# A streaming-encoder block on one Trainium2 core: the residual kept in HBM, and two pairs of buffers for the raw splits

## The chip, the cores and the metric

The kernel runs on one core of a Trainium2 chip. The metric is device time in microseconds (us) of one execution, the median of several runs. Lower is better. The engines have short names in the profile: PE is TensorE's matrix multiplication, PEld its loading of weights, DVE is VectorE, ACT is ScalarE, POOL is GpSimd, and SP (SyncE) issues nearly all of the DMA transfers.

## The reference

One encoder layer works on `x`, 256 frames of 2048 float32 values. It adds five terms to a running sum, the residual, one after the other:

```
x = x + 0.5 * swiglu(rms_norm(x, ffn1_norm), ffn1_w_gate, ffn1_w_up, ffn1_w_down)
proj = rms_norm(x, mix_norm) @ w_in
x = x + concat(pool_mixer(...), gla_mixer(...)) @ w_out
x = x + mem_cross_attention(rms_norm(x, xattn_norm), rms_norm(mem, mem_norm), w_q, w_kv, w_o)
x = x + 0.5 * swiglu(rms_norm(x, ffn2_norm), ffn2_w_gate, ffn2_w_up, ffn2_w_down)
out = rms_norm(x, final_norm)
```

`swiglu` is `(silu(h @ w_gate) * (h @ w_up)) @ w_down`, with a hidden width of 5632. All is float32, and the weights are some 400 MB that are read once each.

## The kernel before

**Units.** Every weight matrix is cut into units of 1 MB, tiles of 128x2048 float32. A unit is loaded into one of three buffers `raw`. Since TensorE is fed with a shorter type (`fp32r`), each unit is split into a high half `wh`, which ScalarE casts (L216), and a low half `wl`, which VectorE makes as the difference (L217). There are three buffers of each. Activations are split alike: `xs` holds the halves of the normed residual, `ys` those of the hidden state or of a mixer's output. One float32 product then becomes three matrix products (`products`, L284, matmul in L289): high by high, high by low, low by high. A plain unit is 24 matmuls of 128x512.

**The order.** `Stream` (L34) holds all 378 units and the small operations between them in program order. `emit` (L65) splits a unit two units ahead of its use, and when unit u is split it issues the load of unit u + 3. A small operation is put into the stream with a delay, counted in units (`op`, L55). The tile framework then plans each engine's order from this program, so the order on an engine is not always that of the program; every engine works its own queue off in order.

**Seven-product units.** Three of the eight units of a gate or up block (numbers 0, 2 and 4, `PAIRS` in L597) use a scheme with seven products in the place of eight: 21 matmuls instead of 24 (`seven`, L367, matmul in L383). It needs sums of weights, which VectorE adds into a tile `T` (`add_weights`, L341), and sums of activations, `xe` (`part_sums`, L323). `split_seven` (L352) makes `wh` and `wl` from `T`. Three of the seven products, P1, P2 and P3, use weights themselves, so a second pair of halves, `xh` and `xl`, is split from three quarters of `raw` (128x1536; these are the raw splits). There is one buffer of each. This second split is a function `rest`, which `emit` keeps in a list `late` and calls when it comes to the next unit; the load of unit u + 3 is issued only after it. In P1, P2 and P3 `xh` is used first and `xl` second. A block of such units (`block_s`, L388) takes all four PSUM tiles; at its end `combine` and `join` (L421, L432) add the seven results up in a tile `sg`.

**The stages.** FFN1 goes through the hidden width in three parts of 4, 4 and 3 blocks of 512 columns (`FF_PARTS`, L595). In each part pairs of blocks are computed, gate first and up second. After the up block the hidden state of the pair is turned: TensorE transposes it into a PSUM tile `ph` (L643), and ACT and DVE split it into `ys`. In a part with two pairs, the first pair is turned during the second pair's up block (the delay is in L658). At the end of each part the down projection adds it to the residual. The mixer follows, then its output projection, cross attention and its output projection, FFN2 in the same three parts, and the final norm.

**The residual.** `X` is one tile in SBUF, 128 partitions by 2 halves of the frames by 2048 values (L167). `load_x` (L524) fills it at the start in eight pieces between the first weight loads. `into_x` (L583) is called for every down projection but the last and for both output projections: two blocks of 1024 columns, each of which is added to `X` (`residual`, L557) from PSUM by VectorE, in two steps of 512 columns. After the last part of a stage `fold` (L566) transposes the new columns on TensorE and splits them into `xs`. `x_chunk` (L535) and `x_squares` (L546) do the same for the start. The last down projection is `down_end` (L1105): `end_evict` (L1134) adds to `X` and multiplies by the final gain into tiles `O`, which have the buffers of `sg`, and `finish` (L1151) scales the rows and stores the output.

Of the kernel before, what the change touches and what calls it, by code (L numbers as in the profile page):

```python
# [7 lines left out]
F32 = mybir.dt.float32  # L8
F32R = mybir.dt.float32r
AF = mybir.ActivationFunctionType  # L10
# [4 lines left out]
P = 128  # L15
D = 2048
S = 256
M = 256
FF = 5632
KT = D // P  # L20
NB = 512
# [71 lines left out]
def build(ctx, tc, I, out):  # L93
    nc = tc.nc
    st = Stream()
# [7 lines left out]
    scope = {"stack": None}  # L103
# [21 lines left out]
    def uid(s):  # L125
        cnt[0] += 1
        return f"{s}{cnt[0]}"
# [36 lines left out]
    sums = ctl("sums", [P, 2])  # L164
    chain = ctl("chain", [P, 2, 8])

    X = main.tile([P, 2, D], F32, tag="X", name="X")  # L167
    xs = main.tile([P, KT, 2, S], F32R, tag="xs", name="xs")
    ys = main.tile([P, KT, 2, S], F32R, tag="ys", name="ys")

# [181 lines left out]
    def split_seven(u, raw, t):  # L352
        th, tl = (
            wpool.tile([P, 4 * NB], F32R, tag=n, name=f"{n}{u}", bufs=st.AHEAD + 1)
            for n in ("wh", "wl")
        )
        split(th, tl, t)
        parts = [x.rearrange("p (b n) -> p b n", n=NB) for x in (th, tl)]

        def rest():  # L360
            r = [scope["pool"].tile([P, 3 * NB], F32R, tag=n, name=f"{n}{u}") for n in ("xh", "xl")]
            split(*r, raw[:, NB:])
            parts.extend(x.rearrange("p (b n) -> p b n", n=NB) for x in r)

        return [parts], rest

    def seven(banks, act, ext, i, g, first, later, weights):  # L367
        th, tl, rh, rl = weights
# [150 lines left out]
    def turn_gains(lo, hi):  # L519
        ps = ptile(uid("pgain"))  # L520
        nc.tensor.transpose(ps[:, 0, :P], rows["gain"], ident)
        nc.vector.tensor_copy(gains[:, lo:hi], ps[:, 0, lo:hi])

    def load_x(c):  # L524
        cols = slice(c * S, (c + 1) * S)
        nc.sync.dma_start(X[:, :, cols], I["x"][0].rearrange("(h p) d -> p h d", p=P)[:, :, cols])

    def first_load_order():
        for c in range(1, 8):
# [2 lines left out]

    first_loads = first_load_order()

    def x_chunk(c):  # L535
        v = ptile(uid("px"))[:, 0, :].rearrange("p (a b) -> p a b", a=2)
        k = 2 * c
        for j in range(2):
            for h in range(2):
                nc.tensor.transpose(  # L540
                    v[:, j, h * P : (h + 1) * P], X[:, h, (k + j) * P : (k + j + 1) * P], ident
                )
        for j in range(2):
            rows["hi", c] = split_scaled(xs, k + j, v[:, j, :], gcol(G_FFN1 + k + j))

    def x_squares(c):  # L546
        with tc.issue_after(rows["hi", c].ins):
            row_squares([X[:, h, c * S : (c + 1) * S] for h in range(2)], c)

    def more_gains():  # L550
        gain_columns(
# [2 lines left out]
             ("gla_b_a", G_BA, 4)], nc.sync,  # L554
        )

    def residual(scale, b):  # L557

        def evict(j, ps):
            x = X[:, :, (2 * b + j) * NB : (2 * b + j + 1) * NB]  # L560
            nc.vector.scalar_tensor_tensor(
                out=x, in0=ps, scalar=scale, in1=x, op0=ALU.mult, op1=ALU.add
            )
        return evict

    def fold(c, gain):  # L566

        v = four(ptile(uid("px")))
        for j in range(4):
            for h in range(2):  # L570
                nc.tensor.transpose(  # L571
                    v[:, j, h * P : (h + 1) * P],
                    X[:, h, c * NB + j * P : c * NB + (j + 1) * P], ident,
                )
        for j in range(4):
            split_scaled(xs, 4 * c + j, v[:, j, :], gcol(gain + 4 * c + j))
        for h in range(2):
            q = tmp.tile([P, NB], F32, tag="j", name=uid("j"), bufs=2)
            nc.scalar.activation(
                q, X[:, h, c * NB : (c + 1) * NB], AF.Square, accum_out=ss[:, h, c : c + 1]  # L580
            )

    def into_x(w, act, scale, gain=None, k0=0, nk=KT, spread_too=True):  # L583

        for b in range(2):
            block_t(wwide(w, b * 2 * NB, k0, nk), act, residual(scale, b))
            if gain is not None:
                for j in range(2):
                    st.op(lambda c=2 * b + j: fold(c, gain), 1)
        if gain is not None:  # L590
            st.op(lambda: finish_norm(4, spread_too), 2)
            if spread_too:
                st.op(spread_norm, 3)
# [81 lines left out]
        st.op(lambda c=c: x_squares(c), 6)  # L675
    st.op(lambda: finish_norm(8, False), 7)
    st.op(more_gains, 8)
    st.op(lambda: turn_gains(G_MIX, G_END), 20)

    def down_first(wd, k0, nk, last):  # L680
        into_x(wd, ys, 0.5, G_MIX if last else None, k0, nk)

    for g in PAIRS:
        pair_sums(g, 5)
# [408 lines left out]
    fin = {}  # L1093
# [11 lines left out]
    def down_end(wd, k0, nk):  # L1105

        acc_ps, kept = {}, []

        def mm(b, k, h, wh, wl):

            wh, wl = (w.rearrange("p (k j n) -> p k j n", j=2, n=NB) for w in (wh, wl))
            for j in range(2):
                nb = 2 * b + j
                if nb not in acc_ps:
                    acc_ps[nb] = ptile(uid("pe"))
                for kk in range(2):
                    products(acc_ps[nb][:, h, :], ys, k + kk, h, wh[:, kk, j], wl[:, kk, j],
                             k + kk == 0, k + kk == nk - 1)
                if k == nk - 2:
                    end_evict(nb, h)  # L1120

        def unit(b, k):
            def fn(wh, wl):
                for h in range(2):
                    mm(b, k, h, wh, wl)
            return fn

        def end_unit(b):
            def fn(wh, wl):
                kept.append((wh, wl))  # L1130
                mm(b, nk - 2, 0, wh, wl)
            return fn

        def end_evict(nb, h):  # L1134
            cols = slice(nb * NB, (nb + 1) * NB)
            if h == 0 and nb % 2 == 0:
                e = scope["pool"].tile([P, 4, NB], F32, tag="sg", name=uid("O"), bufs=2)
                fin[nb], fin[nb + 1] = e[:, 0:2], e[:, 2:4]
            xn, o = X[:, h, cols], fin[nb][:, h, :]
            nc.vector.scalar_tensor_tensor(  # L1140
                out=xn, in0=acc_ps[nb][:, h, :], scalar=0.5, in1=xn, op0=ALU.mult, op1=ALU.add
            )
            nc.scalar.activation(o, xn, AF.Square, accum_out=ss[:, h, nb : nb + 1])
            if nb < 3 or h == 0:
                nc.gpsimd.tensor_tensor(out=o, in0=xn, in1=fin["gB"][:, cols], op=ALU.mult)

        def row_factor(h):
            nc.vector.tensor_reduce(out=sums[:, h : h + 1], in_=ss[:, h, :4], axis=AX.X, op=ALU.add)
            rsqrt(Rcol[:, h : h + 1], sums[:, h : h + 1], D, 1)

        def finish(h, c, engine=None):  # L1151
            cols = slice(c * NB, (c + 1) * NB)
            x, o, r = fin[c][:, h, :], X[:, h, cols], Rcol[:, h : h + 1]
            if h == 1 and c == 3:
                nc.vector.scalar_tensor_tensor(
                    out=o, in0=o, scalar=r, in1=fin["gB"][:, cols], op0=ALU.mult, op1=ALU.mult
                )
            elif engine is nc.scalar:
                nc.scalar.activation(o, x, AF.Copy, scale=r)
            else:  # L1160
                nc.vector.tensor_scalar_mul(o, x, r)
            nc.sync.dma_start(out[0, h * P : (h + 1) * P, cols], o)

        def second_half():
            row_factor(0)
# [12 lines left out]

        st.op(ready_sqrt, 8)
        st.op(last_gain, 2)  # L1180
        for b in range(2):
            for i, src in enumerate(wwide(wd, b * 2 * NB, k0, nk - 2)):
                st.unit(src, unit(b, 2 * i))
        for b in range(2):
            st.unit(wwide(wd, b * 2 * NB, k0 + nk - 2, 2)[0], end_unit(b))
        st.op(second_half)
# [73 lines left out]
```

## Time and profile before

| | |
|---|---|
| three runs | median 2155.78 us, from 2154.47 to 2157.33 |
| the profiled execution | 2156.07 us |
| its span in the profile | 2154.2 us |
| mean granted clock of TensorE | 0.996 of full speed |
| DVE, wait of the `xl` split for the cast of `xh` | 3.7 us, 8 times |
| HBM | 400.80 MB read, 2.10 MB written |

The profile is of one execution. The span runs from the first to the last recorded instruction; the 1.9 us beside it lie around it. A page gives the busy time of each engine with its share of the span, the groups of instructions (line, engine, operation, tile written <- tiles read, shape, count, then busy us, mean ns of one, and the idle time just before them with what ended it) and the DMA queues (packets, MB, share of the DMA engines). Views of the trace give waits (engine, tile and line <- engine, tile and line that released it: us in total, times, longest), single instructions in order of time (start in us, length in us, then the instruction, with the idle time before it in brackets), busy time by stretches of the span, and the chain of work that ended last. Line numbers are those of the kernel. The clock in such a view is the one that the throttle granted TensorE, as a share of full speed.

### The profile page before, as it was taken

What the parts mean: (1) busy time and instruction counts of PE and PEld (TensorE: products, weight loads), DVE (VectorE), ACT (ScalarE), POOL (GpSimd) and SP (SyncE); (2) the same over time, 40 slices, a digit from 0 to 9 for tenths busy, and PEclk for the clock granted to TensorE, in tenths of its full rate; (3) what the DMA queues carried; (4) which work ended last, traced back from release to release, by engine and by line L of the source; (5) the groups of instructions that cost most, each with busy time, mean ns of one, the idle gap of its engine ahead of it and who ended that gap; (6) DMA issues with size and microseconds to landing.
All of it is one profiled execution on the core that took longest, in us unless ns stands there. A gap on an engine that the chain in (4) does not pass through costs nothing.

```text
span 2154.2 us, 23983 instructions
## 1 busy us (share of the span) xinstructions
PE 2122.0 (99%) x10032; PEld 1771.5 (82%) x10032; DVE 1428.1 (66%) x1189; ACT 1007.4 (47%) x890; POOL 14.1 (1%) x41
## 2 busy tenths in 40 slices
PE   9999999999999999999999999999999999999998
PEld 7878888788888888888888888888878887888886
DVE  8786588756865576565665545567874888658744
ACT  7453354533543545445445434445543445434433
POOL 0000000000000000000000000000000000000001
PEclk9999999999999999999999999999999999999999
DMA  7555555555565555556555555555556554665653
GB/s 274 176 195 200 210 176 192 192 189 192 188 212 186 182 170 179 172 177 198 189 182 166 168 175 157 181 190 197 174 195 195 198 193 170 201 195 197 227 181 117
DMA packets 134675, 404.44 MB, mean 188 GB/s; under 512 B 8868, under 2 KB 12040, under 8 KB 134184
## 3 DMA queue, kind: packets, MB, share of 16 engines
q1 hardware_dynamic: 134536, 402.92, 55.8%
q8 instruction: 78, 1.28, 0.2%
q14 instruction: 29, 0.24, 0.0%
q10 hardware_dynamic: 32, 0.01, 0.0%
HBM read 400.80 MB, written 2.10 MB: 187 GB/s over the span
## 4 chain that ended last, share of the span: by engine, by line
PE 92%; DVE 5%; issue 2%; ACT 1%; DMA 1%; SPq 0%; DVEq 0%; ACTq 0%
PE pt L289 54%; PE pa L274 15%; PE pt L383 10%; PE pb L289 6%; PE pe L289 3%; DVE wl L217 2%; ACT wh L216 1%; PE ph L643 1%; DVE xl L217 1%; DVE T L345 1%; PE pl L1036 1%; PE pv L1071 1%; PE px L571 0%; DVE sg L434 0%; DMA raw<-in_ffn_w_gate 0%
## 5 line engine op out<-in xcount | busy, mean ns | idle before, releaser
L217 DVE TENSOR_TENSOR wl<-raw,wh 128x2048 fp32r<-128x2048 f32 (+2 forms) x328 | 740.2, 2258 | 530.9 <-ACT wh L216 529.9
L216 ACT CAST wh<-raw 128x2048 fp32r<-128x2048 f32 (+2 forms) x329 | 618.4, 1881 | 671.7 <-PE pt L289 471.4
L289 PE MATMUL pt<-wh,xs 128*128 128x512 f32 x1952 | 616.6, 390 | 0.0
L289 PE MATMUL pt<-wh,ys 128*128 128x512 f32 x1728 | 534.6, 389 | 0.0
L289 PEld LDWEIGHTS pt<-wh,xs 128*128 128x128 f32 x1952 | 366.6, 188 | 76.0
L289 PE MATMUL pt<-wl,xs 128*128 128x512 f32 x976 | 380.6, 390 | 0.0
L289 PEld LDWEIGHTS pt<-wh,ys 128*128 128x128 f32 x1728 | 324.1, 188 | 67.0
L289 PE MATMUL pt<-wl,ys 128*128 128x512 f32 x864 | 336.4, 389 | 0.0
L274 PE MATMUL pa<-xs,wh 128*128 128x512 f32 x896 | 318.4, 399 | 1.7 <-DVE t L248 1.7
L274 PE MATMUL pa<-xs,wl 128*128 128x256 f32 x896 | 249.3, 281 | 0.0
L289 PEld LDWEIGHTS pt<-wl,xs 128*128 128x128 f32 x976 | 183.6, 188 | 37.7
L274 PEld LDWEIGHTS pa<-xs,wh 128*128 128x128 f32 x896 | 168.4, 189 | 41.0 <-issue 2.0
L216 ACT CAST wh<-T 128x2048 fp32r<-128x2048 f32 x54 | 103.1, 1909 | 190.0 <-DVE T L349 148.6
L289 PEld LDWEIGHTS pt<-wl,ys 128*128 128x128 f32 x864 | 162.2, 188 | 33.5
L217 DVE TENSOR_TENSOR wl<-T,wh 128x2048 fp32r<-128x2048 f32 x54 | 123.8, 2292 | 88.9 <-ACT wh L216 88.9
L274 PEld LDWEIGHTS pa<-xs,wl 128*128 128x128 f32 x896 | 169.8, 190 | 1.6 <-issue 0.2
L289 PE MATMUL pb<-wh,xs 128*128 128x512 f32 x384 | 121.7, 392 | 0.5 <-DVE ys L209 0.5
L383 PE MATMUL pt<-wh,xe 128*128 128x512 f32 x324 | 114.5, 394 | 2.1 <-DVE ys L217 2.1
L216 ACT CAST xh<-raw 128x1536 fp32r<-128x1536 f32 x54 | 80.0, 1482 | 52.5 <-PE pt L383 22.1
L217 DVE TENSOR_TENSOR xl<-raw,xh 128x1536 fp32r<-128x1536 f32 x54 | 94.6, 1753 | 4.0 <-ACT xh L216 3.7
L289 PEld LDWEIGHTS pb<-wh,xs 128*128 128x128 f32 x384 | 72.1, 188 | 15.6 <-DVE ys L209 0.7
L383 PE MATMUL pt<-xh,xs 128*128 128x512 f32 x216 | 80.3, 396 | 1.5 <-DVE ys L217 1.5
(202 smaller groups left out, 1674.0 us busy)
## 6 DMA issues: line engine op xcount, KB each, us to landing
raw<-in_ffn_w_down SPq DMA_DIRECT2D x88, 1024.0 KB, 5.4
raw<-in_ffn_w_up SPq DMA_DIRECT2D x80, 1024.0 KB, 5.1
raw<-in_ffn_w_gate SPq DMA_DIRECT2D x77, 1024.0 KB, 5.1
raw<-in_w_in SPq DMA_DIRECT2D x32, 1024.0 KB, 5.2
raw<-in_xattn_w_kv SPq DMA_DIRECT2D x32, 1024.0 KB, 5.3
raw<-in_w_out SPq DMA_DIRECT2D x16, 1024.0 KB, 5.6
raw<-in_xattn_w_q SPq DMA_DIRECT2D x16, 1024.0 KB, 5.1
raw<-in_xattn_w_o SPq DMA_DIRECT2D x16, 1024.0 KB, 5.7
```

What stands on the lines that cost most here:

```text
L216: nc.scalar.copy(hi, src)
L217: nc.vector.tensor_tensor(out=lo, in0=src, in1=f32(hi), op=ALU.subtract)
L274: nc.tensor.matmul(o, w, x, start=k == 0 and i == 0, stop=last and i == 1)
L289: nc.tensor.matmul(ps, a, w, start=first and i == 0, stop=last and i == 2)
L345: nc.vector.tensor_tensor(out=v[:, 0:2], in0=w[:, 1:3], in1=w[:, 0:1].to_broadcast([P, 2, NB]), op=ALU.add)
L383: nc.tensor.matmul(banks[n], x, w, start=first and j == 0, stop=not later and n in ("P1", "P5", "P6", "P7") and j == 2,)
L643: nc.tensor.transpose(v[:, i, h * P : (h + 1) * P], g[:, h, i * P : (i + 1) * P], ident)
L1036: nc.tensor.matmul(ps[:, t, :M], ys[:, 4 * h + d, a, tok], xa["K"][:, d, b, :], start=i == 0, stop=i == 11,)
L1071: nc.tensor.matmul(ps[:, d, :S], xa["V"][:, m, a, col], xa["PT"][:, m, b, :], start=i == 0, stop=i == 5,)
```

## The change

Two things change together. The residual becomes two DRAM tiles of 256 x 1024. A block of columns lives in SBUF only while it is worked on: `fetch_x` reads it into a tile with the tag `sg` (two buffers, shared with the hidden state and the sums of the seven-product blocks) by two transfers of 0.5 MB, two units into the block's own units, and `store_x` writes it back by two transfers after the second addition. The first part of FFN1 fetches from the input `x` instead. The final outputs `O` take the buffers of `xh` and `xl`. And `xh` and `xl` have two buffers each; they are split at once with `wh` and `wl` of the same unit, not later, so that `late` stays empty. One small operation is delayed by 22 units instead of 20.

```diff
-    X = main.tile([P, 2, D], F32, tag="X", name="X")
+    X = [dram.tile([S, 2 * NB], F32, tag=f"X{b}", name=f"X{b}") for b in range(2)]
...
-        def rest():
-            r = [scope["pool"].tile([P, 3 * NB], F32R, tag=n, name=f"{n}{u}") for n in ("xh", "xl")]
+        if True:
+            r = [
+                scope["pool"].tile([P, 3 * NB], F32R, tag=n, name=f"{n}{u}", bufs=2)
+                for n in ("xh", "xl")
+            ]
             split(*r, raw[:, NB:])
             parts.extend(x.rearrange("p (b n) -> p b n", n=NB) for x in r)
-        return [parts], rest
+        return [parts], None
...
+    def x_tile(b):
+        xrows[b] = scope["pool"].tile([P, 2, 2 * NB], F32, tag="sg", name=uid("x"), bufs=2)
+        return xrows[b]
...
+    def fetch_x(b, src=None):
+        t = x_tile(b)
+        for h in range(2):
+            rows_h = slice(h * P, (h + 1) * P)
+            nc.sync.dma_start(
+                t[:, h], X[b][rows_h, :] if src is None else src[rows_h, b * 2 * NB : (b + 1) * 2 * NB]
+            )
+
+    def store_x(b):
+        for h in range(2):
+            nc.sync.dma_start(X[b][h * P : (h + 1) * P, :], xrows[b][:, h])
+
     def residual(scale, b):
         def evict(j, ps):
-            x = X[:, :, (2 * b + j) * NB : (2 * b + j + 1) * NB]
+            x = x_cols((2 * b + j) * NB, NB)
             nc.vector.scalar_tensor_tensor(
                 out=x, in0=ps, scalar=scale, in1=x, op0=ALU.mult, op1=ALU.add
             )
+            if j:
+                store_x(b)
...
         for b in range(2):
+            st.op(lambda b=b: fetch_x(b, src), 2)
             block_t(wwide(w, b * 2 * NB, k0, nk), act, residual(scale, b))
...
-    st.op(lambda: turn_gains(G_MIX, G_END), 20)
+    st.op(lambda: turn_gains(G_MIX, G_END), 22)
...
-        into_x(wd, ys, 0.5, G_MIX if last else None, k0, nk)
+        into_x(wd, ys, 0.5, G_MIX if last else None, k0, nk, src=None if k0 else I["x"][0])
...
-            if h == 0 and nb % 2 == 0:
-                e = scope["pool"].tile([P, 4, NB], F32, tag="sg", name=uid("O"), bufs=2)
-                fin[nb], fin[nb + 1] = e[:, 0:2], e[:, 2:4]
-            xn, o = X[:, h, cols], fin[nb][:, h, :]
+            if h == 0:
+                t = scope["pool"].tile([P, 3 * NB], F32, tag=("xh", "xl")[nb % 2], name=uid("O"), bufs=2)
+                fin[nb] = t[:, : 2 * NB].rearrange("p (h n) -> p h n", h=2)
+            xn, o = x_cols(nb * NB, NB)[:, h], fin[nb][:, h]
...
         st.op(last_gain, 2)
+        for b in range(2):
+            st.op(lambda b=b: fetch_x(b), 1 + 2 * b)
```

More of the change, by code (lines that the diff above doesn't have):

```diff
@@ L165, in build @@
     chain = ctl("chain", [P, 2, 8])
-    X = main.tile([P, 2, D], F32, tag="X", name="X")
+    dram = ctx.enter_context(tc.tile_pool(name="dram", bufs=1, space=bass.MemoryType.DRAM))
+    X = [dram.tile([S, 2 * NB], F32, tag=f"X{b}", name=f"X{b}") for b in range(2)]
     xs = main.tile([P, KT, 2, S], F32R, tag="xs", name="xs")
@@ L522, in turn_gains @@
         nc.vector.tensor_copy(gains[:, lo:hi], ps[:, 0, lo:hi])
+    xrows = {}
+    def x_tile(b):
+        xrows[b] = scope["pool"].tile([P, 2, 2 * NB], F32, tag="sg", name=uid("x"), bufs=2)
+        return xrows[b]
     def load_x(c):
-        cols = slice(c * S, (c + 1) * S)
-        nc.sync.dma_start(X[:, :, cols], I["x"][0].rearrange("(h p) d -> p h d", p=P)[:, :, cols])
+        b = c // 4
+        if c % 4 == 0:
+            x_tile(b)
+        at = (c % 4) * S
+        nc.sync.dma_start(
+            xrows[b][:, :, at : at + S],
+            I["x"][0].rearrange("(h p) d -> p h d", p=P)[:, :, c * S : (c + 1) * S],
+        )
     def first_load_order():
@@ L533, in build, with x_cols @@
     first_loads = first_load_order()
+    def x_cols(c, n):
+        b = c // (2 * NB)
+        return xrows[b][:, :, c - b * 2 * NB : c - b * 2 * NB + n]
     def x_chunk(c):
@@ L540, in x_chunk @@
                 nc.tensor.transpose(
-                    v[:, j, h * P : (h + 1) * P], X[:, h, (k + j) * P : (k + j + 1) * P], ident
+                    v[:, j, h * P : (h + 1) * P], x_cols((k + j) * P, P)[:, h], ident
                 )
@@ L547, in x_squares @@
         with tc.issue_after(rows["hi", c].ins):
-            row_squares([X[:, h, c * S : (c + 1) * S] for h in range(2)], c)
+            row_squares([x_cols(c * S, S)[:, h] for h in range(2)], c)
     def more_gains():
@@ L555, in more_gains @@
         )
+    def fetch_x(b, src=None):
+        t = x_tile(b)
+        for h in range(2):
+            rows_h = slice(h * P, (h + 1) * P)
+            nc.sync.dma_start(
+                t[:, h], X[b][rows_h, :] if src is None else src[rows_h, b * 2 * NB : (b + 1) * 2 * NB]
+            )
+    def store_x(b):
+        for h in range(2):
+            nc.sync.dma_start(X[b][h * P : (h + 1) * P, :], xrows[b][:, h])
     def residual(scale, b):
         def evict(j, ps):
-            x = X[:, :, (2 * b + j) * NB : (2 * b + j + 1) * NB]
+            x = x_cols((2 * b + j) * NB, NB)
             nc.vector.scalar_tensor_tensor(
@@ L568, in fold @@
         v = four(ptile(uid("px")))
+        x = x_cols(c * NB, NB)
         for j in range(4):
@@ L571, in fold @@
                 nc.tensor.transpose(
-                    v[:, j, h * P : (h + 1) * P],
-                    X[:, h, c * NB + j * P : c * NB + (j + 1) * P], ident,
+                    v[:, j, h * P : (h + 1) * P], x[:, h, j * P : (j + 1) * P], ident
                 )
@@ L578, in fold, with into_x @@
             q = tmp.tile([P, NB], F32, tag="j", name=uid("j"), bufs=2)
[L579 to L583, printed above, removed]
+            nc.scalar.activation(q, x[:, h], AF.Square, accum_out=ss[:, h, c : c + 1])
+    def into_x(w, act, scale, gain=None, k0=0, nk=KT, spread_too=True, src=None):
         for b in range(2):
+            st.op(lambda b=b: fetch_x(b, src), 2)
             block_t(wwide(w, b * 2 * NB, k0, nk), act, residual(scale, b))
@@ L1152, in finish @@
             cols = slice(c * NB, (c + 1) * NB)
-            x, o, r = fin[c][:, h, :], X[:, h, cols], Rcol[:, h : h + 1]
+            x, o, r = fin[c][:, h], x_cols(c * NB, NB)[:, h], Rcol[:, h : h + 1]
             if h == 1 and c == 3:
```

## The prediction

> **What bounds the kernel now.** I read the page first, then TensorE's waits, then busy time by stretch, then the rows of one stretch. From the page:
>
> ```profile
> PE 2122.0 (99%) x10032; PEld 1771.5 (82%) x10032; DVE 1428.1 (66%) x1189; ACT 1007.4 (47%) x890; POOL 14.1 (1%) x41
> ...
> q1 hardware_dynamic: 134536, 402.92, 55.8%
> ...
> L216 ACT CAST wh<-raw 128x2048 fp32r<-128x2048 f32 (+2 forms) x329 | 618.4, 1881 | 671.7 <-PE pt L289 471.4
> ...
> raw<-in_ffn_w_down SPq DMA_DIRECT2D x88, 1024.0 KB, 5.4
> ```
>
> TensorE is busy for 2122.0 of the 2154.2 us of the span, so 32.2 us is all that any rearrangement can win by filling its gaps. The DMA engines are used to 55.8%, and the casts that fill `wh` mostly wait for TensorE to give a buffer back, not for weights. So the question is which of the 32 us are waits that this change touches. The waits, TensorE's and, for comparison, two of ScalarE's (us in total, times, longest):
>
> ```profile
> ACT xh L216 <- PE pt L383: 22.1, 18, 2.6
> ...
> ACT xh L216 <- DMA raw<-in_ffn_w_up: 19.7, 8, 3.1
> ...
> PE pt L383 <- DVE xl L217: 10.7, 5, 2.9
> ...
> PE pt L383 <- DVE ys L217: 3.6, 4, 2.1
> ```
>
> Line 383 is the matmul of the seven-product units, and `xl` is the low half of their raw splits, the tile that gets a second buffer. It is the largest wait on TensorE: 10.7 us in 5 waits, with 3.6 us more for `ys`. ScalarE's cast of `xh` waited 18 times for TensorE to finish with the single buffer, and 8 times for its weights. Busy time by stretch (columns: PE, PEld, DVE, ACT, POOL, granted clock, DMA share, GB/s) shows where:
>
> ```profile
> 100.00:160.00 60.00, 56.09 (x254) 45.48 (x253) 48.46 (x38) 32.19 (x23) 0.00 (x0) 1.00 0.50 175
> 370.00:420.00 50.00, 46.53 (x205) 37.47 (x206) 41.43 (x31) 25.32 (x19) 0.00 (x0) 0.98 0.57 195
> 1512.00:1570.00 58.00, 54.54 (x241) 43.79 (x241) 47.26 (x36) 30.64 (x22) 0.00 (x0) 0.98 0.50 170
> 1775.00:1832.00 57.00, 53.52 (x239) 42.99 (x238) 47.24 (x36) 29.71 (x22) 0.00 (x0) 0.99 0.48 167
> 160.00:272.00 112.00, 112.00 (x504) 93.01 (x503) 68.84 (x43) 44.50 (x26) 0.00 (x0) 1.00 0.57 197
> 414.80:417.60 2.80, 0.00 (x0) 0.00 (x0) 2.80 (x3) 0.00 (x0) 0.00 (x0) 1.00 0.60 152
> 418.00:421.30 3.30, 3.30 (x9) 2.61 (x8) 1.22 (x3) 2.30 (x2) 0.00 (x0) 0.50 0.98 379
> 2145.00:2154.20 9.20, 0.00 (x0) 0.00 (x0) 3.60 (x11) 2.00 (x6) 1.27 (x1) 0.69 0.61 228
> ```
>
> The first four stretches are the same place four times: the up block of a second column pair, in the first two parts of both feed-forward stages, where the hidden state of the pair before is turned as well. TensorE lacks 3.9, 3.5, 3.5 and 3.5 us in them, 14.4 together. The fifth is a down stage: TensorE never idles. The last is the tail of the kernel; the change adds nothing to its chain, so its 9.2 us stay.
>
> After the 2.90 us stall that ends at 417.62 the granted clock is 0.50 through the seventh stretch. Half speed costs half of its 3.3 us, 1.7 us, on top of the idle time. The trace's 0.98 and 0.99 in stretches two to four are the same thing once in each; the first stretch, whose stalls are 2.11 and 1.76, shows 1.00. [...]
>
> **Why TensorE waits there.** DVE, then ACT, in the second stretch; the second ACT row is the cast of `xh`:
>
> ```profile
> 385.41 2.29 DVE L217 TENSOR_TENSOR wl<-raw,wh 128x2048 fp32r<-128x2048 f32 x1 [0.15 <-ACT wh L216]
> ...
> 397.74 1.22 DVE L434 TENSOR_TENSOR sg<-pt,sg 128x1024 f32<-128x1024 f32 x1 [3.17 <-PE pt L289]
> 398.88 2.28 DVE L217 TENSOR_TENSOR wl<-T,wh 128x2048 fp32r<-128x2048 f32 x1
> ...
> 403.28 1.22 DVE L217 TENSOR_TENSOR ys<-ph,ys 128x1024 fp32r<-128x1024 f32 x1
> ...
> 410.27 2.29 DVE L217 TENSOR_TENSOR wl<-T,wh 128x2048 fp32r<-128x2048 f32 x1 [2.06 <-ACT wh L216]
> 412.48 2.28 DVE L217 TENSOR_TENSOR wl<-raw,wh 128x2048 fp32r<-128x2048 f32 x1
> 414.68 1.22 DVE L345 TENSOR_TENSOR T<-raw 128x1024 f32<-128x1024 f32 x1
> 415.81 1.75 DVE L217 TENSOR_TENSOR xl<-raw,xh 128x1536 fp32r<-128x1536 f32 x1
> ```
>
> ```profile
> 394.65 1.91 ACT L216 CAST wh<-T 128x2048 fp32r<-128x2048 f32 x1 [2.30 <-DVE T L349]
> ...
> 411.95 1.47 ACT L216 CAST xh<-raw 128x1536 fp32r<-128x1536 f32 x1
> ```
>
> ```profile
> 404.55 0.50 PE L383 MATMUL pt<-xh,xs 128*128 128x512 f32 x1 [0.52 <-DVE ys L217]
> ...
> 417.62 0.53 PE L383 MATMUL pt<-xl,xs 128*128 128x512 f32 x1 [2.90 <-DVE xl L217]
> ```
>
> While DVE idles for 3.17 us before 397.74 it could have made this `xl`, but its buffer still holds the unit before. The write comes 18 us later, behind two `wl` and a `T` (queues are in order), and TensorE stands from 414.72 to 417.62.
>
> **The change part by part.** *Second pair of xh and xl.* Instruction counts on TensorE, DVE and ScalarE are unchanged; the order is not. In the changed order of DVE the `xl` of the second seven-product unit stands before the `wl` of the first. Its weights were loaded behind the third `wl` before (about 387.6, two units back) and land after about 5.4, by 393; the cast takes 1.47, to about 394.7; `xl` 1.75, to 396.4: inside the 3.17 us in which DVE idled. The first `wl` then starts at 396.6, where its cast (394.65 to 396.56, now a little behind `xh`) ends, and not at 398.88. Running the rest of the changed order with the rows' lengths (wl 2.2, sg, T and ys 1.14 each, the short sums 0.6): sg to 399.9, wl 402.1, T 403.2, ys 404.3, sg 405.5, T ready 406.7, cast 1.9, second-unit `wl` at about 411. TensorE needs that at 414, and the `xl` is long there. So the 2.90 and its 1.7 of clock go. The 0.52 before 404.55 goes too: `ys` ends no later, and three products of the later unit are ordered ahead of the wait. That is 5.1 us. What is late next is the third unit's `wl`, at about 421.7, against a need of about 423.5. The third and fourth stretches are ordered alike and have the same rows:
>
> ```profile
> 1554.34 0.50 PE L383 MATMUL pt<-xh,xs 128*128 128x512 f32 x1 [0.49 <-DVE ys L217]
> ...
> 1567.41 0.50 PE L383 MATMUL pt<-xl,xs 128*128 128x512 f32 x1 [2.87 <-DVE xl L217]
> ...
> 1817.25 0.50 PE L383 MATMUL pt<-xh,xs 128*128 128x512 f32 x1 [0.52 <-DVE ys L217]
> 1830.32 0.50 PE L383 MATMUL pt<-xl,xs 128*128 128x512 f32 x1 [2.90 <-DVE xl L217]
> ```
>
> 0.49 + 2.87 + 1.7 and 0.52 + 2.90 + 1.7 give 5.1 and 5.1. The first stretch has two stalls:
>
> ```profile
> 142.80 0.50 PE L383 MATMUL pt<-wh,xe 128*128 128x512 f32 x1 [2.11 <-DVE ys L217]
> ...
> 155.74 0.50 PE L383 MATMUL pt<-xl,xs 128*128 128x512 f32 x1 [1.76 <-DVE xl L217]
> ```
>
> The 1.76 goes for the same reason. The 2.11 is a wait for a PSUM bank that `ys` frees; in the new order `xl` goes into an idle gap, `ys` is only some 0.4 earlier, and three more products (0.7) precede the wait: I keep 1.0 of it. That is 1.1 + 1.8 = 2.9.
>
> *What the new order costs.* ScalarE's queue is in order, and some `xh` casts now stand ahead of a `wh` cast that TensorE needs sooner. The worst place is the second pair's start in the second part:
>
> ```profile
> 365.82 2.29 DVE L217 TENSOR_TENSOR wl<-T,wh 128x2048 fp32r<-128x2048 f32 x1 [2.05 <-ACT wh L216]
> ```
>
> The `wl` at 365.82 ended at 368.1. It gets one more `xl` (1.75) and some 1.0 of waiting for that `xh` ahead of it: about 370.8. TensorE starts that pair at 356.92 and has 58 products before it needs it:
>
> ```profile
> 356.92 0.39 PE L383 MATMUL pt<-xh,xs 128*128 128x512 f32 x1
> ```
>
> ```profile
> 169.00 24.26 PE pt L289 x107
> ```
>
> By the second row (of the chain that ended last) a product takes 24.26 / 107 = 0.227, so the need is at 370.1: a new stall of 0.7, in both feed-forward stages, 1.4 in all. Bounds, by the rows: 0 where the load lands in time, 2.9 with a half-clock window (4.6) where it does not. I take 0.7, from the chain itself.
>
> *Residual in HBM.* SP issues 60 more transfers of 0.5 MB: 32 fetches and 28 stores, 31.5 MB on 402.92, so the DMA share goes from 56% to about 60% and in a down stage from 0.57 to about 0.71. Nothing on TensorE reads them directly except the transposes of the fold, a unit after the add. A fetch is issued about six units (6 x 24 x 0.227 = 33 us) before its add, against 5.4 for 1 MB: hidden. The one wait in SP's order is at the first down units: the fetch needs the buffer of the hidden state, which TensorE frees when it turns it. The SP rows (from a load's issue on) and the chain:
>
> ```profile
> 191.45 3.97 SPq L471 DMA_DIRECT2D raw<-in_ffn_w_down  x2
> ```
>
> ```profile
> 193.25 1.75 PE ph L643 x16
> ```
>
> ```profile
> 203.44 1.91 ACT L216 CAST wh<-raw 128x2048 fp32r<-128x2048 f32 x1 [3.53 <-PE pt L289]
> ```
>
> The fetch cannot go before 195.0, and the weight load issued at 191.45 is behind it: 3.6 of waiting, about 0.7 for two more issues, 1 MB ahead of it in the one queue at most 5.4, charged in full: 10 us late. It landed at about 196.9 and was cast at 203.44, for a unit that TensorE starts at about 214: cast and `wl` take 4.2, so 13 us late would be just in time. Cost taken: 0. Without that cover it would be 1 us on TensorE for each us beyond. The stores stand behind the add that feeds them, and in DVE's order the add stands before the `wl` that releases the next load, so they hold up nothing. [...]
>
> *The sum.* 2.9 + 5.1 + 5.1 + 5.1 = 18.2 won, 1.4 lost: 16.8 us. The profiled execution took 2156.07 (1.9 around its span); less 16.8 it is 2139.3. The median of the three runs shown is 2155.78, 0.3 below it. I say **2139.5**.
>
> **The rivals.**
> - *Early casts block the queue (gain halved).* If the loads behind the early `xh` casts land 2 us later than 5.4, the `wh` casts behind them move, and the start of each pair's second block stalls: 4 or 5 places with 1 to 2 us each. For: `xh` is the one cast that already waited for loads. Against: most places have 2 to 3 us of cover. 2139.5 + 8 = 2147, up to 2153.
> - *The change doesn't remove the wait.* DVE is busy for 41.43 of 50 us there; if the backlog and not the buffer is the cause, `xl` is made early and something else is late by as much, and the time is 2154 to 2157. Against: DVE's own 3.17 us of idle time just ahead.
> - *SP is held up (slower).* One mechanism: at the eight blocks of down projections that start behind a turned or freed buffer, the fetch stands at SP's head and weight loads wait. It decides from 13 us of lateness on, 3 more than worked out. At 2 us beyond it, each of 8 places loses 2 + 1.7 of clock, 30 us, against the 16.8 won: 2169. Against: the stretch 160 to 272, with TensorE full and casts that wait for TensorE.
>
> **How the numbers follow.** Forecast (2134 to 2147) 0.62; first rival (2147 to 2153) 0.15; no effect 0.10; slower 0.13. All FFN stalls gone with their clock would be 2156.07 - 14.4 - 5.1 = 2136.6; the changed schedule may also move the small gaps of the mixer by 2 us, so the low end is 2134. The high end takes in the first rival, 2153; what is left out is some 0.2. A measurement of this kernel tells about 0.2% (4.3 us) from no change: faster than that 0.75 (the forecast and most of the first rival), within it 0.12, slower 0.13.
>
> **What would show each step.** Right: TensorE's waits for `xl` and the four gaps shrink to about 1 us in each stretch, no 0.50 clock there, `xh` no longer waits for TensorE; about 434 MB in the queue. Wrong: waits of line 383 on `wl` or on the casts at the start of second blocks; weight casts that wait for DMA in the down stages; TensorE idle there at all. The prediction falls if idle time on TensorE stays above 25 us in all.

## The result, and the profile after

The changed kernel takes 2137.71 us (median of four runs, 2136.34 to 2138.64) against 2155.83 for the kernel before: a ratio of 0.9915, 95% interval 0.9898 to 0.9932. The forecast was 2139.5, with a range of 2134 to 2147. The profiled executions are 2138.64 and 2156.07, 17.4 apart, and the spans 2136.9 and 2154.2.

From the page of the changed kernel; the line numbers of the matmuls and splits are two to five higher than before (L216 and L217 are now L218 and L219, L289 is L291, L383 is L388):

```profile
PE 2115.0 (99%) x10032; PEld 1769.1 (83%) x10032; DVE 1425.8 (67%) x1189; ACT 1006.0 (47%) x890; POOL 14.2 (1%) x41
...
q1 hardware_dynamic: 143176, 434.38, 60.1%
...
HBM read 417.58 MB, written 16.78 MB: 203 GB/s over the span
```

TensorE's span minus its busy time went from 32.2 to 21.9 us, which is 10.3 of the 17.3. The other 7.0 are busy time, mostly products that no longer run at half clock: the trace of before has four windows of 0.50 ahead of its tail, each 3.41 us long, that of the changed kernel one, and three times half of 3.41 is 5.1. The queue moved the 31.5 MB more that were counted from the code. The waits of the changed kernel (us in total, times, longest):

```profile
ACT xh L218 <- DMA raw<-in_ffn_w_gate: 36.6, 16, 4.8
ACT xh L218 <- DMA raw<-in_ffn_w_up: 36.1, 19, 5.1
...
ACT xh L218 <- PE pt L388: 25.7, 6, 10.6
...
PE pt L291 <- ACT wh L218: 1.7, 2, 0.8
PE pt L388 <- DVE ys L219: 1.7, 3, 0.7
```

No wait of TensorE for `xl` is left in the list, where 10.7 us stood. The cast of `xh` is now mostly ahead of its weights: it waits 35 times for a load, and TensorE never for `xh`. One sign that the prediction named for being right did not show: the cast still waits for TensorE, 25.7 us in 6 waits, where it was 22.1 us in 18. The four stretches again (columns as before):

```profile
100.00:160.00 60.00, 59.26 (x271) 48.88 (x270) 50.86 (x40) 33.05 (x23) 0.00 (x0) 1.00 0.60 205
...
370.00:420.00 50.00, 49.46 (x226) 40.78 (x225) 42.27 (x32) 28.07 (x21) 0.00 (x0) 1.00 0.62 210
...
1512.00:1570.00 58.00, 57.62 (x263) 47.55 (x262) 48.88 (x36) 30.91 (x23) 0.00 (x0) 1.00 0.57 190
...
1775.00:1832.00 57.00, 57.00 (x260) 47.17 (x259) 49.19 (x36) 32.36 (x23) 0.00 (x0) 1.00 0.63 214
```

TensorE lacks 0.74, 0.54, 0.38 and 0 us, 1.7 together instead of 14.4, and the granted clock is 1.00 in all four. What it still waits for, from the rows of its products in time:

```profile
141.68 0.50 PE L388 MATMUL pt<-wh,xe 128*128 128x512 f32 x1 [0.74 <-DVE ys L219]
...
367.30 0.49 PE L291 MATMUL pt<-wh,xs 128*128 128x512 f32 x1 [0.84 <-ACT wh L218]
...
402.21 0.50 PE L388 MATMUL pt<-xh,xs 128*128 128x512 f32 x1 [0.54 <-DVE ys L219]
...
743.22 0.50 PE L276 MATMUL pa<-xs,wh 128*128 128x512 f32 x1 [0.44 <-DVE xs L211]
...
1771.40 0.49 PE L291 MATMUL pt<-wh,xs 128*128 128x512 f32 x1 [0.84 <-ACT wh L218]
```

Both traces have 10032 matmuls, so the start of the n-th in one can be set against the n-th in the other. The distance grows in a few places only:

| place (products, time before) | forecast | measured |
|---|---|---|
| first stretch (400 to 800, 94 to 187) | -2.9 | -3.8 |
| start of the second pair, part two (1600 to 1800) | +0.7 | +0.85 |
| second stretch (1800 to 2000) | -5.1 | -5.15 |
| start of the mixer (3200 to 3400) | 0 | +0.8 |
| third stretch (7200 to 7600) | -5.1 | -5.7 |
| start of the second pair, FFN2 (8400 to 8600) | +0.7 | +0.65 |
| fourth stretch (8600 to 8800) | -5.1 | -5.1 |
| sum of all | -16.8 | -17.4 |

### The profile page after: what moved, and what is told of

The parts are those of the page before. It is cut to its first block, busy times and chain, and to the rows that moved or that the text cites. A ratio compares the mean times of both kernels' runs of the same rounds, so it can differ in the third digit from the quotient of the medians.

```text
span 2136.9 us, 24071 instructions
## 1 busy us (share of the span) xinstructions
PE 2115.0 (99%) x10032; PEld 1769.1 (83%) x10032; DVE 1425.8 (67%) x1189; ACT 1006.0 (47%) x890; POOL 14.2 (1%) x41
## 4 chain that ended last, share of the span: by engine, by line
PE 97%; DVE 2%; ACT 1%; issue 0%; DMA 0%; SPq 0%; DVEq 0%; ACTq 0%
PE pt L291 58%; PE pa L276 15%; PE pt L388 12%; PE pb L291 6%; PE pe L291 3%; ACT wh L218 1%; PE ph L678 1%; DVE wl L219 1%; PE pl L1071 1%; PE pv L1106 1%; PE px L608 0%; DMA x<-in_x 0%; PE px L562 0%; PE po L941 0%; DVE sg L439 0%
## 5 line engine op out<-in xcount | busy, mean ns | idle before, releaser
L219 DVE TENSOR_TENSOR wl<-raw,wh 128x2048 fp32r<-128x2048 f32 (+2 forms) x328 | 739.8, 2258 | 515.5 <-ACT wh L218 515.1
L218 ACT CAST wh<-raw 128x2048 fp32r<-128x2048 f32 (+2 forms) x329 | 618.4, 1881 | 626.3 <-PE pt L291 415.4
L291 PE MATMUL pt<-wh,xs 128*128 128x512 f32 x1952 | 620.1, 390 | 1.7 <-ACT wh L218 1.7
L291 PE MATMUL pt<-wh,ys 128*128 128x512 f32 x1728 | 534.5, 389 | 0.0
L291 PEld LDWEIGHTS pt<-wh,xs 128*128 128x128 f32 x1952 | 366.4, 188 | 78.1 <-ACT wh L218 2.5
L291 PE MATMUL pt<-wl,xs 128*128 128x512 f32 x976 | 380.4, 390 | 0.0
L291 PEld LDWEIGHTS pt<-wh,ys 128*128 128x128 f32 x1728 | 324.1, 188 | 66.8
L291 PE MATMUL pt<-wl,ys 128*128 128x512 f32 x864 | 336.3, 389 | 0.0
L291 PEld LDWEIGHTS pt<-wl,xs 128*128 128x128 f32 x976 | 183.5, 188 | 37.9
L291 PEld LDWEIGHTS pt<-wl,ys 128*128 128x128 f32 x864 | 162.2, 188 | 33.6
L218 ACT CAST wh<-T 128x2048 fp32r<-128x2048 f32 x54 | 103.1, 1909 | 171.1 <-DVE T L351 162.7
L219 DVE TENSOR_TENSOR wl<-T,wh 128x2048 fp32r<-128x2048 f32 x54 | 123.8, 2293 | 86.4 <-ACT wh L218 86.0
L218 ACT CAST xh<-raw 128x1536 fp32r<-128x1536 f32 x54 | 80.1, 1483 | 98.6 <-DMA raw<-in_ffn_w_gate 36.6
L291 PE MATMUL pb<-wh,xs 128*128 128x512 f32 x384 | 121.7, 392 | 0.5 <-DVE ys L211 0.5
L388 PE MATMUL pt<-wh,xe 128*128 128x512 f32 x324 | 109.5, 390 | 0.8 <-DVE ys L219 0.7
L219 DVE TENSOR_TENSOR xl<-raw,xh 128x1536 fp32r<-128x1536 f32 x54 | 94.8, 1755 | 15.8 <-ACT xh L218 15.5
L291 PEld LDWEIGHTS pb<-wh,xs 128*128 128x128 f32 x384 | 72.1, 188 | 15.6 <-DVE ys L211 0.7
L388 PE MATMUL pt<-xh,xs 128*128 128x512 f32 x216 | 79.5, 391 | 0.9 <-DVE ys L219 0.9
```

Source lines behind the costliest of these rows:

```text
L218: nc.scalar.copy(hi, src)
L219: nc.vector.tensor_tensor(out=lo, in0=src, in1=f32(hi), op=ALU.subtract)
L291: nc.tensor.matmul(ps, a, w, start=first and i == 0, stop=last and i == 2)
L388: nc.tensor.matmul(banks[n], x, w, start=first and j == 0, stop=not later and n in ("P1", "P5", "P6", "P7") and j == 2,)
```

## The experiments

In all of them the time beside "before" is that of the kernel before on the same chip in the same job. The first question was which part of the change does it.

**Only the residual in HBM.** The changed kernel with the old `split_seven`, and two more tiles for `O`:

```diff
-                scope["pool"].tile([P, 3 * NB], F32R, tag=n, name=f"{n}{u}", bufs=2)
-        return [parts], None
+            r = [scope["pool"].tile([P, 3 * NB], F32R, tag=n, name=f"{n}{u}") for n in ("xh", "xl")]
+        return [parts], rest
```

> Only the residual in HBM: xh and xl have one buffer each and are split late, as before; the 60 fetches and stores stay. Theory (the second pair of buffers does it all, the residual only makes room and costs nothing): about 2156 (2153 to 2159), with TensorE's five waits for xl back at about 10.7 us, three stalls of 2.9 and three half-clock windows. Rival (the residual's traffic or the new tiles for x move the time themselves): more than 4 us away from the kernel before, or xl's waits below 6 us.

2159.10 against 2157.59, ratio 1.0003 (0.9994 to 1.0012). The waits of this run for comparison:

```profile
ACT xh L218 <- PE pt L385: 22.6, 17, 2.6
...
PE pt L385 <- DVE xl L219: 12.4, 6, 2.9
```

So the residual in HBM alone neither wins nor costs, and the waits are back. What it brings is 16 KB of SBUF per partition.

**Two buffers, split late.** The same, with `bufs=2` in the late split:

> The changed kernel, but the raw splits are traced late, as before, with two buffers. Theory A (the single buffer held the split back; with a second one the planner may move it up by itself): 2136 to 2141. Theory B (the position in the program does it, the buffer alone not): 2148 to 2156, with waits for xl above 5 us.

2135.91 against 2157.59, ratio 0.9900 (0.9885 to 0.9914). Theory A: the place in the program does not matter, the planner moves the split up as soon as a buffer allows it. In this trace the second unit's `xl` of the second stretch stands here, where it was at 415.81 before:

```profile
391.77 1.75 DVE L219 TENSOR_TENSOR xl<-raw,xh 128x1536 fp32r<-128x1536 f32 x1
```

**Early split, late load.** `return [parts], lambda: None` keeps the load one unit late.

> The changed kernel, but the load of unit u + 3 is still issued one unit later behind a seven-product unit, as before; the raw splits are made at once. Theory (the early split does it, not the earlier load): 2136 to 2142. Rival (the earlier load is what makes room for the early split): xh waits longer for its weights, TensorE's waits for xl or wl return, 2145 to 2153.

2137.08 against 2157.59, ratio 0.9906 (0.9889 to 0.9922). The load's place does not matter either.

**No traffic for the residual.**

```diff
+        if "short" in rows and "last" not in rows:
+            return rows["short"][:, :, c % NB : c % NB + n]
...
     def store_x(b):
-        for h in range(2):
-            nc.sync.dma_start(X[b][h * P : (h + 1) * P, :], xrows[b][:, h])
+        return
```

> The changed kernel without the residual's traffic: one SBUF tile of 512 columns stands for all of the residual, so nothing is fetched or stored but the two blocks of the end (the sums are then wrong ones; all instructions on TensorE, VectorE and ScalarE stay). Theory (fetches and stores are hidden): 2136 to 2139, equal to the changed kernel within its noise. Rival (the traffic delays weight loads and costs something already): 2125 to 2134, with fewer waits for raw.

2136.29 against 2157.59, ratio 0.9903 (0.9888 to 0.9917). Within the noise it is the changed kernel, so the fetches and stores are hidden. How far they are from being seen, the next two tell.

**One and three MB more behind each fetch.** After each transfer of `fetch_x` stand one, or three, transfers of 0.5 MB to a DRAM tile that nothing reads:

```diff
+            for i in range(1):
+                with tc.issue_after(got.ins):
+                    d = dram.tile([P, 2 * NB], F32, tag=uid("d"), name=uid("d"))
+                    nc.sync.dma_start(d, I["x"][0][rows_h, b * 2 * NB : (b + 1) * 2 * NB])
```

> The changed kernel with 1 MB of idle transfers (HBM to HBM, never read) queued behind each fetch of a block, twice the fetch's own traffic. In the profile of the changed kernel the weight load behind the second fetch landed 6.6 us after its issue, 1.4 us before its cast, and that cast waits for TensorE with a unit to spare: some 11 us of cover. Theory (cover): 2 MB more are at most 10.8 us more, so 2136 to 2142. Rival (SP or the queue is at its limit): 2145 or more.

2136.76 against 2156.56, ratio 0.9906 (0.9890 to 0.9923).

> The same with 3 MB of idle transfers behind each fetch. Theory (cover of some 11 us per place): 6 MB for the two fetches of a stage take 16 to 32 us, beyond the cover by 5 to 20 us in some seven places: 2170 to 2280, with weight casts that wait for raw in the down stages. Rival (the DMA engines are used to 60% only, so the traffic stays hidden at any such amount): below 2146.

2193.01 against 2156.56, ratio 1.0172 (1.0157 to 1.0188). The first down stage of this run, on ScalarE and TensorE:

```profile
225.21 1.90 ACT L218 CAST wh<-raw 128x2048 fp32r<-128x2048 f32 x1 [13.76 <-DMA raw<-in_ffn_w_down]
```

```profile
227.16 1.22 PE L291 MATMUL pt<-wh,ys 128*128 128x512 f32 x2 [6.20 <-ACT wh L218]
```

The mechanism of the slower rival exists: a cast that waits for its weights, and TensorE that waits for the cast. It begins between 1 and 3 MB beyond the change's own traffic behind a fetch, and then costs some 55 us. The idle transfers go from HBM to HBM and not into SBUF, so the point need not be the same for fetches.

**Which of the two buffers.** The prediction spoke of `xl`, because TensorE waits for `xl`. Each of the two alone, split late:

```diff
-            r = [scope["pool"].tile([P, 3 * NB], F32R, tag=n, name=f"{n}{u}", bufs=2) for n in ("xh", "xl")]
+            r = [scope["pool"].tile([P, 3 * NB], F32R, tag=n, name=f"{n}{u}", bufs=2 if n == "xh" else 1)
+                 for n in ("xh", "xl")]
```

> The raw splits traced late, two buffers for xh and one for xl. Theory (xl's single buffer is the wait, since TensorE waits for xl): nearly nothing is won, 2150 to 2158, with TensorE's waits for xl at 8 us or more. Rival (the single xh blocked ScalarE's queue, 22.1 us of waits, and that made the backlog): 2138 to 2146.

2136.47 against 2156.41, ratio 0.9904 (0.9890 to 0.9919). The theory falls: the whole gain is there with a single `xl`. The converse (`"xl"` for `"xh"` in the condition):

> The converse of the run before: one buffer for xh, two for xl, split late. The first theory (xl's single buffer is the wait) fell, since with xl single and xh doubled the time was 2136.5. Theory now (the xh cast has to wait until TensorE is through with the xh before, and stands in ScalarE's queue behind two wh casts by then; xl follows from it): nothing is won, 2153 to 2160, TensorE's waits for xl at 8 us or more. Rival (either second buffer is enough, since both are read by the same products): 2136 to 2142.

2158.89 against 2157.52, ratio 1.0004 (0.9995 to 1.0014). With one `xh` a second `xl` is worth nothing, and TensorE's wait for `xl` is back:

```profile
PE pt L385 <- DVE xl L219: 11.0, 9, 2.9
```

ScalarE in the second stretch of that run:

```profile
411.07 1.91 ACT L218 CAST wh<-T 128x2048 fp32r<-128x2048 f32 x1 [1.32 <-DVE T L351]
412.88 1.91 ACT L218 CAST wh<-raw 128x2048 fp32r<-128x2048 f32 x1
414.69 1.47 ACT L218 CAST xh<-raw 128x1536 fp32r<-128x1536 f32 x1
```

It is the order of before, shown here, in which `xh` comes behind the two `wh`, and `xl` cannot be made ahead of `xh`:

```profile
408.32 1.91 ACT L216 CAST wh<-T 128x2048 fp32r<-128x2048 f32 x1 [1.32 <-DVE T L349]
410.13 1.90 ACT L216 CAST wh<-raw 128x2048 fp32r<-128x2048 f32 x1
411.95 1.47 ACT L216 CAST xh<-raw 128x1536 fp32r<-128x1536 f32 x1
```

With two `xh` and one `xl`, ScalarE, then VectorE:

```profile
390.50 1.49 ACT L218 CAST xh<-raw 128x1536 fp32r<-128x1536 f32 x1 [1.20 <-DMA raw<-in_ffn_w_up]
```

```profile
406.30 1.75 DVE L219 TENSOR_TENSOR xl<-raw,xh 128x1536 fp32r<-128x1536 f32 x1
```

`xl` is still made late, but not behind a cast, and its end at 408.1 is enough. Its buffer now makes VectorE wait, 15.7 us in 14 waits. TensorE waits for `xl` 1.1 us in the whole trace, and not at all in this stretch:

```profile
DVE xl L219 <- PE pt L385: 15.7, 14, 2.0
...
PE pt L385 <- DVE xl L219: 1.1, 3, 0.8
```

```profile
383.00:418.00 35.00, 35.00 (x164) 29.15 (x163) 31.02 (x23) 19.10 (x15) 0.00 (x0) 1.00 0.51 181
```

**The two stalls of 0.84.** The prediction had them at 0.7. In the changed kernel ScalarE does this ahead of the first:

```profile
362.15 1.48 ACT L218 CAST xh<-raw 128x1536 fp32r<-128x1536 f32 x1 [10.60 <-PE pt L388]
363.54 1.91 ACT L218 CAST wh<-T 128x2048 fp32r<-128x2048 f32 x1
365.35 1.90 ACT L218 CAST wh<-raw 128x2048 fp32r<-128x2048 f32 x1
```

`xh` of a later unit stands ahead of two `wh` that TensorE needs sooner; the last ends at 367.25, and the product at 367.30 waits for it. (With two `xh` and one `xl` no such stall is in the trace: TensorE has no wait for `wh` there.) The late split with two buffers, and one `xh` put behind the `wh` cast of the unit before it:

```diff
+                if g == pairs[1] and gate:
+                    hold.add(len(st.units))
...
+            if u in hold:
+                with tc.issue_after(casts[u - 1].ins):
+                    split(*r, raw[:, NB:])
```

> The raw splits traced late with two buffers, and in the first half of each gate block the cast of xh is put behind the wh cast of the unit before it. Theory (the two stalls of 0.84 at 367 and 1768 come from that xh cast, which waits for its weights ahead of two weight casts that are ready): both go, 1.7 us less than with the late split alone, 2134.2. Rival (the casts wait for something else there, or the later xl stalls its own products): 2135.5 to 2139.

2137.66 against 2156.56, ratio 0.9910 (0.9896 to 0.9925), and both stalls are there, 0.83 each. The attempt settles nothing about the theory: I had counted one unit off, and the `xh` in the way is that of the third seven-product unit. With `pairs[2]`:

> The raw splits traced late with two buffers; this time the xh cast of the third seven-product unit of a gate block stands behind the wh cast of the unit before it (in the last attempt it was the second unit's, and the cast that stood in the way in both stalls was the third's: unit 68 ahead of the weights of 66 and 67). Theory: both stalls of 0.84 go, and nothing else moves: 1.7 less than the late split alone (2135.9), about 2134. Rival (VectorE's backlog makes the weights late there anyway): the stalls stay, 2135 to 2138.

2135.93 against 2156.41, ratio 0.9902 (0.9888 to 0.9917). Both stalls are gone from the trace, so the cause is shown. The time is no better than that of the late split alone, though: the profiled execution had another stall in the first stretch, with a half-clock window behind it:

```profile
142.93 0.50 PE L392 MATMUL pt<-wh,xe 128*128 128x512 f32 x1 [2.07 <-DVE ys L219]
```

```profile
143.90:147.20 3.30, 3.30 (x9) 2.55 (x9) 2.52 (x4) 1.97 (x3) 0.00 (x0) 0.50 0.33 132
```

The same edit in the changed kernel itself:

> The changed kernel, split at once, with the same placing of the third unit's xh cast. Theory: the two stalls of 0.84 go, 1.7 less than the changed kernel: about 2136 where the mixer's half-clock window falls in, 2134.3 where it does not. Rival: the stalls stay, 2137 to 2139.

2134.73 against 2156.41, ratio 0.9897 (0.9881 to 0.9914). ScalarE at the place:

```profile
362.21 1.91 ACT L218 CAST wh<-T 128x2048 fp32r<-128x2048 f32 x1 [10.08 <-DVE T L352]
364.03 1.91 ACT L218 CAST wh<-raw 128x2048 fp32r<-128x2048 f32 x1
365.83 1.48 ACT L218 CAST xh<-raw 128x1536 fp32r<-128x1536 f32 x1
```

Both stalls are gone. It has the lowest median of all kernels tried; the step from the changed kernel, 3.0 us by the medians of two jobs, is not clear of the noise, since the intervals of the two ratios overlap.

**What calls half clock.** 35 stalls of seven lengths, made on TensorE:

```diff
+        tc.keep_in_program_order(
+            nc.tensor.matmul(ps[:, 0, :32], ones, Z[:, :32], start=True, stop=True)
+        )
+        n = LENGTHS[stalls[0] % len(LENGTHS)]
+        stalls[0] += 1
+        while n:
+            nc.gpsimd.memset(Z[:, : min(n, NB)], 0.0)
+            n -= min(n, NB)
+        return nc.tensor.matmul(ps[:, 0, :32], ones, Z[:, :32], start=True, stop=True)
```

> The changed kernel with 35 stalls made on TensorE in the down blocks and output projections: a small product, a GpSimd memset of one of seven lengths behind it, a small product that reads it. It shows which idle time is followed by half clock. Theory (a grid): the records decide in fixed windows of 3.413 us, and a window with about 1.65 us or more of idle time on TensorE is followed by one at half clock, wherever the stall lies in it: stalls of 1.7 to 2.9 us are then punished in some places and not in others, by how a window's border cuts them, and the rule holds for every window. Rival (a length): every stall above some 2.5 us is punished and none below.

One execution took 2200.27 us, the stalls included. They came out shorter than meant, up to 2.04. Two of them, and the stretches right behind them (the last columns: clock, DMA share, GB/s):

```profile
980.31 0.41 PE L308 MATMUL pz<-Z,ones 128*128 128x32 f32 x2 [1.59 <-POOL Z L306]
```

```profile
1009.75 0.41 PE L308 MATMUL pz<-Z,ones 128*128 128x32 f32 x2 [2.04 <-POOL Z L306]
```

```profile
981.00:984.20 3.20, 3.20 (x9) 2.55 (x8) 2.44 (x2) 0.03 (x1) 0.00 (x0) 0.50 0.50 148
...
1011.70:1014.90 3.20, 3.20 (x16) 2.64 (x15) 0.13 (x1) 0.00 (x0) 0.00 (x0) 1.00 0.60 142
```

The shorter one was punished, the longer one not: length does not decide. By the clock records, whose windows are 3.413 us long on one grid, the 1.59 lay within one window and the 2.04 was cut by a border into 0.45 and 1.59. The theory is borne out only in part. Three made stalls of 1.65 within one window (they end at 491.40, 1051.17 and 1416.76) were followed by half clock too, and in this kernel no window with less than 1.59 us of idle time was. But the second part of the 2.04 is also 1.59 in one window, and was not punished. Nor does a single threshold hold over the other kernels: a window with 1.92 with three MB more, the start of the stall of 6.20, was not punished. Nor was this stall with one `xh`, which a border cuts into 1.74 and 1.15; the second row is the stretch behind it:

```profile
420.36 0.51 PE L385 MATMUL pt<-xl,xs 128*128 128x512 f32 x1 [2.89 <-DVE xl L219]
```

```profile
422.60:425.90 3.30, 3.30 (x16) 2.75 (x15) 2.21 (x2) 3.30 (x3) 0.00 (x0) 1.00 0.64 257
```

In every trace the half-clock records lie on one grid (in that of before 147, 337 and 414 lengths of 3.413 us behind the first); what else decides stays open.

## Why the prediction was right, and where it was not

- *The stalls of the second column pair go.* Right in place and nearly in size: 18.2 won by the forecast, 19.8 by the table. Their share of half clock, 1.7 for each of three windows (half of 3.41 us, an estimate from the granted 0.50), came as charged: the clock is 1.00 in all four stretches. The sum is closer than its terms, and that is luck: 1.6 more was won and 0.9 more lost than forecast.
- *Why they go.* Here a step failed. "While DVE idles for 3.17 us before 397.74 it could have made this `xl`, but its buffer still holds the unit before": the runs show that `xl`'s buffer is not what mattered, 2136.5 with two `xh` and one `xl`, 2158.9 the other way round. The tile that held all back is `xh`. TensorE's products read it, so with one buffer the next cast needs it back from them; the rows of before have that cast behind two `wh` in ScalarE's order, and `xl` follows from `xh`. The row named the last link of the chain, and the prediction took it for the first. ScalarE's 22.1 us of waits of `xh` for TensorE, quoted beside it, would not have told: the same wait is 21.7 us with two `xh` and one `xl`, where the gain is whole, and 20.3 with one `xh`, where there is none. What differs is the place of the cast in ScalarE's order, which the planner sets; why it sets it so is argued from the rows and not tested. That the time came out right all the same is luck: the change doubles both.
- *The 0.52 ahead of 404.55.* It was to go and stayed, 0.54 at 402.21. `ys` ends 2.3 us earlier than before, but TensorE comes 3.0 us earlier, and the three products ordered ahead of the wait (0.7) are used up by that. In the third stretch 0.38 of the 0.49 stayed, in the fourth the 0.52 went.
- *The first stretch.* 1.0 was kept of the 2.11; the profile has 0.74.
- *The early `xh` casts.* 0.7 was charged twice; the trace has 0.85 and 0.65 by the distance of the products, and taking the `xh` cast out of the way took both stalls away. That cast waited 10.60 us for TensorE to give a buffer back, not for its load, from which the forecast drew its bounds. ScalarE did keep its order here: the `wh` cast at 374.49 had by the semaphores nothing left to wait for from 370.17 on, and stood behind that of 372.67, for whose `T` ScalarE idled 5.43 us. The forecast had TensorE wait for a `wl`, the trace has it wait for the `wh` of a plain unit in the same queue. The first rival's "4 or 5 places" were these two.
- *The residual's traffic.* Zero was right, and the lateness behind it was not. Read wrongly was "the weight load issued at 191.45 is behind it", for which "10 us late" was charged. SP in the changed kernel:

```profile
187.57 0.38 SPq L476 DMA_DIRECT2D raw<-in_ffn_w_down  x1
...
191.15 0.33 SPq L583 DMA_DIRECT2D x<-in_x  x1
191.57 0.39 SPq L476 DMA_DIRECT2D raw<-in_ffn_w_down  x1
```

  TensorE had won 3.85 by then. The second fetch's first transfer goes when it was forecast to, at 195.0 less 3.85. But the load of 191.45 is the one at 187.57, ahead of it and on time; it stands behind the first fetch alone, which went out at 185.4, and took 6.6 us instead of 5.0. So with 1 MB ahead of it the load was 1.6 late, and not late by that megabyte's whole length. The load behind the second fetch's first transfer, issued at 191.57, was at 195.06 before, which is 191.2 by the same count: 0.4 late at the issue. SP's wait for the buffer ran beside the load's own wait for `raw`, and was not added to it. (The expectation of the run with 1 MB more gives the 6.6 to this load; it belongs to the load before it.) The 13 us from which the rival decides were not measured; the runs with 1 and 3 MB more do not contradict them.
- *The clock.* That the stalls of 2.87 to 2.90 us were followed by half clock, 1.7 charged for each, held for the profile of before, but not as a rule of length: the 2.89 with one `xh` was followed by a clock of 1.00, and of the made stalls the 1.59 by 0.50.
- *Not foreseen.* 0.8 at the start of the mixer, where the order of the norm's splits changed (0.44 of it is the stall at 743.22). It returns, at 0.44 to 0.45, in all kernels with the residual in HBM, and is missing where nothing is fetched or stored.

## What to carry to other kernels

A wait names the last tile of a chain; before a buffer is doubled, follow the chain back through the engine that makes the tile and ask which earlier tile's buffer held its maker up. Then double each buffer alone: here half of the added buffers, the 6 KB per partition of `xh`, did all the work. Traffic moved to HBM cost nothing here (2137.7 us with it, 2136.3 without) while the loads behind it kept their cover, and the cover is best measured by adding dummy transfers until the time moves. The price of a short stall on TensorE was not its length alone here: behind the 2.11 of before the clock stayed at 1.00, behind the 2.07 above it was 0.50 through a stretch of 3.30 us, some 1.7 on top (half of it, an estimate).

## What the runs showed of the hardware

The trace of before has a granted clock of 0.50 in four windows of 3.413 us, from 417.96, 919.72, 1568.26 and 1831.08, whole numbers of windows apart (147, 337 and 414 behind the first), and once more at its end, from 2148.52 on; the changed kernel has it from 912.73 for 3.413 us, and from 2131.28 on. By the clock such a window costs half its length, 1.7 us; this is an estimate, beside which 9 products in 3.20 us at 0.50 stand against 16 at 1.00 in the kernel with the made stalls. The two stalls of 1.01 and 1.65 in the mixer are the same in all 14 traces of this study. Where the 1.65 lies within one window of the grid it was followed by half clock in seven traces of eight (the changed kernel and the one before among them), and in none of the six where a border cuts it (the late split and the kernel without traffic among them); the mean clock of the profiled execution is 0.998 in the changed kernel and 0.999 in the late split and without traffic. So two executions of nearly the same schedule can differ by such a window, an estimated 1.7 us, for no reason in the schedule, and differences of that size between these kernels are not to be read from one profile.
